# Gated delta rule: decay matrices summed in PSUM by one-hot products of split gates, beta in the exponent, one product for both decayed matrices, normalisation of two pairs at once

## The chip, the cores and the metric

The kernel runs on one core of a Trainium2 chip. The metric is the device time of one execution in microseconds (us), the median over the runs shown. A core has a matrix engine (TensorE, in the rows PE, its weight loads PEld), an elementwise engine (VectorE, DVE), an engine for functions of one operand (ScalarE, ACT), a general one (GpSimd, POOL), a queue that issues transfers (SyncE, SP) and 16 DMA engines. Operands lie in SBUF; products land in PSUM.

## The reference, cut to what matters

One layer: a bidirectional gated DeltaNet mixer, a layer norm, a mixture of experts, a second layer norm and a gate. The change lies in the mixer, 16 heads (8 pairs that share q and k), 512 tokens, forward and backward:

```python
gc = jnp.cumsum(g, axis=-1)
decay = jnp.exp(jnp.where(incl, gc[..., :, None] - gc[..., None, :], -jnp.inf))
kb = k * beta[..., None]
lhs = eye + jnp.einsum("nbhik,nbhjk->nbhij", kb, k) * decay * (1.0 - eye)
u = solve(lhs, v * beta[..., None])
w = solve(lhs, kb * jnp.exp(gc)[..., None])
attn = jnp.einsum("nbhik,nbhjk->nbhij", q, k) * decay
...
v_new = u_c - w_c @ state
o     = q_c @ state + attn_c @ v_new
state = state * gl + k_c.T @ v_new
```

After it the heads are normalised (`_rms`), multiplied by silu(z) and projected. The result is the same for both kernels.

## The kernel before

The mixer takes the first 700 us of the span, then come the first layer norm and the routing, from about 760 us the experts, whose 96 weight parts of 1 MB each stream in through a ring, and from about 1010 us the second norm and the gate. The weights of the experts can only begin to load when the mixer has given its memory back.

The mixer uses chunks of 128 tokens (4 of them). Its work goes by quarters `qt` of 2 pairs (4 heads) each:

- `projections` (`do_k`, `do_q`, `do_v`, `do_z` through `project`, L226 to L237): 24 products of 128x512 for each 128 channels, on operands that are split exactly in two fp32r parts. The split of the weights is a copy on ScalarE (L232) and a subtraction on GpSimd (L234). `conv_silu` then runs 4 taps and the silu on VectorE (L251, L255), straight out of PSUM. `do_k` also makes k k^T (L293, copied out at L295 into `kk`), `do_q` makes k q^T (L310, L313, into `kq`).
- `norms(qt)`: reciprocals and square roots per token, and `sc` = beta / |k|^2, `scd` = `sc` e^(gl - gc).
- `solve(qt)`: inverts the 32x32 blocks on the diagonal, one block a partition, by 30 steps of two VectorE operations (L389, L391); `lay(qt)` puts the result into the layouts of the products.
- `build(qt, hf)`: for 2 chunks of each direction, the decay matrices and the two decayed products E (from `kk`, for the inverse) and AT (from `kq`, for the output), then the inverse from 32 to 128 by small products. There are 8 builds. Each has 4 parts (direction, chunk) that make `dc` for 4 heads: a transfer that spreads gc over the partitions (L438), the mask added on GpSimd (L439), 4 exponentials with the bias -gc on ScalarE (L441), 2 products on GpSimd for AT (L445) and 4 on VectorE for E (L449).
- `steps(qt, hf)`: the recurrence, 8 steps for each half quarter; the product with E (L552), its two scaled copies `wd` (L558) and `w` (L562) on ScalarE, the state (L565, L569), the output (L576, L580).
- `finish(p)`: rms norm of a pair (squares L594, `rsqrt` L260 to L267, product L600), then transposes and silu(z).
- `fill`: the output projection of heads 0 to 11, through `project` too, until about 706 us; heads 12 to 15 follow chunk by chunk.

The order on each engine is made ahead of the run by a planner, which simulates the program: `weave` interleaves the parts of steps, build, finish, solve, projections and fill in the program, steps with a higher priority, and the planner takes what is ready on each engine. The engines then run in that fixed order. From the experts on the order is that of the program. The PSUM tag `pmisc` has one buffer; transposes, `kk`, `kq` and `finish` share it. All loads go through SP's one queue.

Of the kernel before, what the change touches and what calls it, by code (L numbers as in the profile page):

```python
# [16 lines left out]
P = 128  # L17
# [33 lines left out]
BKQ = 3  # L51
# [15 lines left out]
def program(ctx: ExitStack, tc: tile.TileContext, a: dict, out: bass.AP):  # L67
# [11 lines left out]
    # ---- constants  # L79
# [12 lines left out]
    # silu(y) = (1 + tanh(y / 2)) y / 2  # L92
    V.tensor_scalar(cvw, cvw, 0.5, None, op0=OP.mult)
    gdnv = c1.tile([P, 2, 32], F32, name="gdnv")
    nc.sync.dma_start(gdnv[:, 0], a["a_log"].to_broadcast([P, 32]))
    nc.sync.dma_start(gdnv[:, 1], a["dt_bias"].to_broadcast([P, 32]))
# [3 lines left out]
    negm = c1.tile([P, 2, P], F32, name="negm")  # L100
# [8 lines left out]
    hd = tr.enter_context(tc.tile_pool(name="hd", bufs=4, side="right"))  # L109
    tr2 = ExitStack()  # L110
# [28 lines left out]
    # ---- gates: g and beta, [tok, chunk, dir, head]  # L139
# [3 lines left out]
    axl = wk.tile([P, 4, NC_, 32], F32, name="th", bufs=BTH)  # L143
    ax, l1, g, gc = (axl[:, i] for i in range(4))
    V.tensor_tensor(ax, pab[:, :, 0:32], gdnv[:, 1:2, :].to_broadcast([P, NC_, 32]), op=OP.add)
# [4 lines left out]
    tmp4 = wk.tile([P, 4, NC_, 32], F32, name="zs")  # L150
    e1, u1, d1 = (tmp4[:, i] for i in range(3))
# [16 lines left out]
    V.tensor_mul(g, l1, nea.to_broadcast([P, NC_, 32]))  # L168

    # e^{gc}, e^{gl-gc}, e^{gl}  # L170
# [9 lines left out]
    ngc = sq("ngc")  # L180
    V.tensor_scalar(ngc, gc, -1.0, None, op0=OP.mult)
# [6 lines left out]
    nc.sync.dma_start(gcd, gcT)  # L188
    A.activation(egc, pg[:, 0], AF.Exp)
    A.activation(egr, pg[:, 1], AF.Exp)  # L190
    A.activation(egl, pg[:, 2], AF.Exp)
    V.tensor_scalar(negc, egc, -1.0, None, op0=OP.mult)
# [12 lines left out]
    for q in range(4):  # L205
        s = slice(32 * q, 32 * q + 32)
        V.tensor_copy(negb[s, 0], negm[s, q // 2, s])
# [5 lines left out]
    sc = sq("sc")  # L213
# [44 lines left out]
    kcm, qcm, ktm, nv, kk, kq = {}, {}, {}, {}, {}, {}  # L258

    def rsqrt(y, x, t):  # L260
        """y = 1 / sqrt(x), by Newton's steps from the exponent's half; x is lost"""
# [7 lines left out]
    def rsqrt1(y, x, t):  # L269
        """the same for one number per partition"""  # L270
# [7 lines left out]
    def do_k(p):  # L278
# [8 lines left out]
        scr = wk.tile([P, P], BF16, name="scr")  # L287
        for c in range(NC_):
            A.activation(scr, ktm[p][:, c], AF.Square, accum_out=nk2[:, c, p:p + 1])
        pk = psum.tile([P, NC_, P], F32, name="pmisc", bufs=1)  # L290
        for c in range(NC_):
            kc = kcm[p][:, c * P:(c + 1) * P]
            T.matmul(pk[:, c], kc, kc, start=(c == 0), stop=True, skip_group_check=True)  # L293
        kk[p] = hd.tile([P, NC_, P], F32, name="kk", bufs=BKK)
        A.activation(kk[p], pk, AF.Copy)  # L295

    def do_q(p):
# [6 lines left out]
        scr = wk.tile([P, P], BF16, name="scr")  # L304
# [3 lines left out]
        pk = psum.tile([P, NC_, P], F32, name="pmisc", bufs=1)  # L308
        for c in range(NC_):
# [1270 lines left out]
```

## Time and profile before

| what | us |
|---|---|
| median of 3 runs | 1121.25 |
| the 3 runs | 1120.5, 1121.25, 1128.5 |
| the profiled execution, span from its first to its last instruction | 1118.7 |
| median less that span | 2.55 |

The profile has no other time of the profiled execution than its span; what lies around it in a run is taken as the 2.55 us between that span and the median. Busy shares over the span: TensorE 90%, VectorE 75%, ScalarE 49%, GpSimd 34%. These are means over stages of different kinds, so the stages are read one by one.

### The profile page before, as it was taken

The page shows a single profiled execution, that of the slowest core. Times are in us where ns is not written, and L with a number is a line of the kernel's source. Part 1 is how long each engine was busy: PE and PEld are TensorE (multiplying, and loading weights), DVE is VectorE, ACT ScalarE, POOL GpSimd, SP SyncE. Part 2 cuts the span into 40 slices and gives each one's busy share as a digit, 9 for nine tenths or more (in the row PEclk, how much of TensorE's full clock was granted, in tenths as well). Part 3 has the DMA queues.
Part 4 walks back from the last instruction along what each step waited for, and adds up shares of the span by engine and source line. Part 5 has one row for each costly group of instructions (what it writes and reads, how often), then busy time and mean ns, then how long its engine had stood idle before and what let it go on. Part 6 is the DMA issues. An engine that isn't in the chain of part 4 may idle for free. (4 is left out here: it accounts for less than half of the span.)

```text
span 1118.7 us, 19886 instructions
## 1 busy us (share of the span) xinstructions
PE 1003.2 (90%) x6954; PEld 696.7 (62%) x6954; DVE 843.1 (75%) x1944; ACT 552.2 (49%) x1420; POOL 380.9 (34%) x337
## 2 busy tenths in 40 slices
PE   8974789887989898889998999958999999999788
PEld 7753668776767677668887887843333333333367
DVE  5899999999897879995756434597666676666794
ACT  3543467656557585735777453124543344432321
POOL 1647544336163446233541265052100000000362
PEclk8987799999899898999999999978999999999899
DMA  4423222122123212413335344868999999991411
GB/s 161 116 84 107 74 83 78 42 64 66 40 76 110 85 47 73 133 59 108 103 101 167 104 128 126 350 223 304 416 420 420 419 399 395 391 374 38 161 57 47
DMA packets 80118, 188.73 MB, mean 169 GB/s; under 512 B 15344, under 2 KB 36848, under 8 KB 67344
## 3 DMA queue, kind: packets, MB, share of 16 engines
q1 hardware_dynamic: 77712, 179.05, 44.2%
q0 software_dynamic: 2304, 8.39, 2.0%
q8 instruction: 55, 0.90, 0.3%
q14 instruction: 47, 0.39, 0.1%
HBM read 174.77 MB, written 12.65 MB: 168 GB/s over the span
## 5 line engine op out<-in xcount | busy, mean ns | idle before, releaser
L234 POOL TENSOR_TENSOR wl<-wr,wh 128x512 fp32r<-128x512 f32 x120 | 160.3, 1340 | 296.2 <-ACT wh L232 130.8
L237 PE MATMUL pin<-xh,wh 128*128 128x512 f32 x448 | 139.5, 427 | 44.7 <-DVE cv L251 28.6
L237 PE MATMUL pin<-xh,wl 128*128 128x512 f32 x448 | 132.3, 411 | 0.9 <-POOL wl L234 0.9
L237 PE MATMUL pin<-xl,wh 128*128 128x512 f32 x448 | 132.8, 414 | 0.0
L237 PEld LDWEIGHTS pin<-xh,wh 128*128 128x128 f32 x448 | 85.5, 199 | 66.2 <-issue 37.1
L232 ACT ACTIVATE wh<-wr 128x512 fp32r<-128x512 f32 x120 | 75.5, 632 | 90.8 <-PE pin L237 44.2
L1209 ACT ACTIVATE ws<-w 128x512 f32 x96 | 60.5, 630 | 112.0 <-PE ps L1214 58.7
L1207 DVE COPY ws<-w 128x512 f32 x288 | 105.6, 423 | 8.9 <-issue 3.0
L237 PEld LDWEIGHTS pin<-xl,wh 128*128 128x128 f32 x448 | 88.1, 200 | 19.0
L251 DVE SCALAR_TENSOR_TENSOR cv<-pin,cvw,cv 128x510 f32<-128x510 f32 (+1 forms) x128 | 94.6, 741 | 4.4 <-ACT cv L248 3.2
L237 PEld LDWEIGHTS pin<-xh,wl 128*128 128x128 f32 x448 | 84.5, 195 | 18.1 <-POOL wl L234 1.5
L943 POOL DMA_INDIRECT E<-x1d,gim x16 | 16.2, 1012 | 170.7 <-PE ps L1197 157.0
L449 DVE SCALAR_TENSOR_TENSOR E<-dc,sc,kk 128x128 f32<-128x128 f32 x128 | 64.9, 561 | 4.5 <-PE ps L552 2.7
L391 DVE TENSOR_TENSOR x<-x,tmp 128x30 f32<-128x30 f32 (+14 forms) x120 | 58.2, 485 | 2.1
L445 POOL TENSOR_TENSOR AT<-dc,kq 128x256 f32<-128x256 f32 x64 | 49.4, 801 | 25.9 <-PE ps L576 21.8
L389 DVE TENSOR_TENSOR tmp<-x 128x30 f32<-128x30 f32 (+14 forms) x120 | 53.8, 448 | 1.7
L1302 DVE SCALAR_TENSOR_TENSOR x<-pin,cq,x 128x512 f32<-128x512 f32 x36 | 26.9, 750 | 36.5 <-PE pin L1297 34.0
L439 POOL TENSOR_TENSOR dc<-dc,negm 128x512 f32<-128x512 f32 x32 | 44.6, 1399 | 18.3 <-DMA dc<-gcd 12.7
L576 PE MATMUL ps<-w,AT 128*128 128x128 f32 x256 | 43.2, 291 | 5.6 <-DVE oacc L580 5.6
L562 ACT ACTIVATE w<-ps,sc 128x128 f32<-128x128 f32 x128 | 40.4, 377 | 14.1 <-PE ps L552 14.0
L254 ACT ACTIVATE th<-cv 128x512 f32<-128x512 f32 x32 | 20.1, 629 | 51.9 <-DVE cv L251 32.8
L576 PEld LDWEIGHTS ps<-w,AT 128*128 128x128 f32 x256 | 39.1, 201 | 9.8 <-DVE oacc L580 6.1
(432 smaller groups left out, 2208.7 us busy)
## 6 DMA issues: line engine op xcount, KB each, us to landing
w<-in_w_gu SPq DMA_DIRECT2D x64, 1024.0 KB, 10.2
w<-in_w_dn SPq DMA_DIRECT2D x32, 1024.0 KB, 10.1
wr<-in_w_in SPq DMA_DIRECT2D x96, 256.0 KB, 2.7
dc<-gcd SPq DMA_DIRECT2D x32, 256.0 KB, 3.5
wr<-in_w_out SPq DMA_DIRECT2D x24, 256.0 KB, 2.7
zd<-th SPq DMA_DIRECT2D x16, 256.0 KB, 2.5
zs<-zd SPq DMA_DIRECT2D x16, 256.0 KB, 2.6
w<-in_pe_g SPq DMA_DIRECT2D x6, 512.0 KB, 6.9
```

The source lines that it names most:

```text
L232: A.activation(wh, wr, AF.Copy)
L234: G.tensor_tensor(wl, wr, wh.bitcast(F32), op=OP.subtract)
L237: T.matmul(ps, w[:, k], parts[k0 + k][n], start=(k0 + k + n == 0 and w is wh), stop=(k0 + k == nk_ - 1 and w is wl))
L251: V.scalar_tensor_tensor(y[:, lo:hi], ps[:, lo + j - 2:hi + j - 2], cvw[:, m, j:j + 1], y[:, lo:hi], op0=OP.mult, op1=OP.add)
L389: V.tensor_tensor(t, X[:, m + 1:, m:m + 1].to_broadcast([P, n, m]), X[:, m:m + 1, :m].to_broadcast([P, n, m]), op=OP.mult)
L391: V.tensor_tensor(X[:, m + 1:, :m], X[:, m + 1:, :m], t, op=OP.add)
L439: G.tensor_tensor(dc, dc, negm[:, d:d + 1].to_broadcast([P, 4, P]), op=OP.add)
L445: G.tensor_tensor(AT[:, k:k + 2], dc[:, 2 * pl:2 * pl + 2], kq[p][:, c:c + 1].to_broadcast([P, 2, P]), op=OP.mult)
L449: V.scalar_tensor_tensor(E[:, k + e], dc[:, 2 * pl + e], sc[:, c, hh:hh + 1], kk[p][:, c], op0=OP.mult, op1=OP.mult)
L576: T.matmul(p3[:, e], AT[:, us + e], w[:, e], start=True, stop=True, skip_group_check=True)
L1207: V.tensor_copy(ws[:, p:p + 1], src)
L1209: A.activation(ws[:, p:p + 1], src, AF.Copy)
```

## The change

The decay matrices are no longer made from transferred rows. The transposed gates are split in two fp32r parts and kept in one tile `ghl` [128, chunk, token]: partitions 0 to 31 the high part of gc, 32 to 63 its low part, 64 to 95 and 96 to 127 the two parts of log(beta), one partition for each direction and head. For each direction and pair of heads a group of 7 products adds up, in one PSUM bank `pd` [128, 2 heads, 2 chunks, 128], the mask, gc of the column token, and -gc + log(beta) of the row token; `sel` are the one-hot columns. One exponential takes all of it to SBUF, and 2 VectorE products multiply it with `kkq`, which holds kk and kq side by side, already divided by |k|^2. beta and 1/|k|^2 are then in E and AT, and `w` is a plain copy.

```diff
+    ghl = hd2.tile([P, NC_, P], F32R, name="ghl", bufs=1)
+    A.activation(ghl[0:32], gcT, AF.Copy)
+    V.tensor_tensor(ghl[32:64], gcT, ghl[0:32].bitcast(F32), op=OP.subtract)
+    ptl = psum.tile([32, NC_, P], F32, name="pmisc", bufs=1)
+    for c in range(NC_):
+        T.transpose(ptl[:, c], l1[:, c, 32:64], ident)
...
+    A.activation(lbT, ptl, AF.Copy, scale=-1.0)
+    A.activation(lbh, lbT, AF.Copy)
+    V.tensor_copy(ghl[64:96], lbh)
+    V.tensor_tensor(ghl[96:128], lbT, lbh.bitcast(F32), op=OP.subtract)
...
     def build(qt, hf, Ec, T32, T64):
-        E = ab_pool.tile([P, 16, P], F32, name="E")
-        AT = ab_pool.tile([P, 16, P], F32, name="AT")
+        EA = [ab_pool.tile([P, 8, 2, P], F32, name=n) for n in ("E", "AT")]
+        E = [t[:, :, 0] for t in EA]
...
-            for cc in range(2):
-                c = c0[d] + cc
-                dc = wk.tile([P, 4, P], F32, name="dc", bufs=3)
-                nc.sync.dma_start(dc, gcd[u0:u0 + 4, c, :][None].to_broadcast([P, 4, P]))
-                G.tensor_tensor(dc, dc, negm[:, d:d + 1].to_broadcast([P, 4, P]), op=OP.add)
-                for u in range(4):
-                    A.activation(dc[:, u], dc[:, u], AF.Exp, bias=ngc[:, c, u0 + u:u0 + u + 1])
-                for pl in range(2):
-                    G.tensor_tensor(AT[:, k:k + 2], dc[:, 2 * pl:2 * pl + 2],
-                                    kq[p][:, c:c + 1].to_broadcast([P, 2, P]), op=OP.mult)
-                    for e in range(2):
-                        V.scalar_tensor_tensor(E[:, k + e], dc[:, 2 * pl + e],
-                                               sc[:, c, hh:hh + 1], kk[p][:, c], op0=OP.mult, op1=OP.mult)
+            for pl in range(2):
+                p = 2 * qt + pl
+                u = 16 * d + 2 * p
+                pd = psum.tile([P, 2, 2, P], F32, name="pmisc", bufs=1)
+                T.matmul(pd.rearrange("p e c i -> p (e c) i"), idr, negm[:, d:d + 1].to_broadcast([P, 4, P]),
+                         start=True, stop=False, skip_group_check=True)
+                for e in range(2):
+                    T.matmul(pd[:, e], sel[:, 0, u + e:u + e + 1].to_broadcast([P, P]), ghl[:, c0[d]:c0[d] + 2],
+                             start=False, stop=False, skip_group_check=True)
+                for k in (1, 2):
+                    for cc in range(2):
+                        T.matmul(pd[:, :, cc], ghl[:, c0[d] + cc], sel[:, k, u:u + 2, None].to_broadcast([P, 2, P]),
+                                 start=False, stop=(k == 2 and cc == 1), skip_group_check=True)
+                dc = wk.tile([P, 2, 2, P], F32, name="dc")
+                A.activation(dc, pd, AF.Exp)
+                for cc in range(2):
+                    k = 4 * cc + 2 * pl
+                    V.tensor_tensor(EA[d][:, k:k + 2], dc[:, :, cc, None, :].to_broadcast([P, 2, 2, P]),
+                                    kkq[p][:, c0[d] + cc][:, None].to_broadcast([P, 2, 2, P]), op=OP.mult)
                 yield
```

Around it: log(beta) comes out of the series that makes the gates, which so runs over 64 columns a chunk instead of 32. The products for `kk` move from `do_k` into `norms`, behind the reciprocals, and both `kk` and `kq` leave PSUM by 4 scaled copies (one a chunk) instead of one:

```diff
+    def products(p, i, r):
+        pk = psum.tile([P, NC_, P], F32, name="pmisc", bufs=1)
+        for c in range(NC_):
+            cs = slice(c * P, (c + 1) * P)
+            T.matmul(pk[:, c], kcm[p][:, cs], r[p][:, cs], start=(c == 0), stop=True, skip_group_check=True)
+        for c in range(NC_):
+            A.activation(kkq[p][:, c, i], pk[:, c], AF.Copy, scale=rk2[:, c, p:p + 1])
...
     def norms(qt):
-                V.tensor_mul(sc[:, :, hs], beta[:, :, hs], rk2[:, :, ps])
-                V.tensor_mul(scd[:, :, hs], sc[:, :, hs], egr[:, :, hs])
+                V.tensor_mul(scd[:, :, hs], begr[:, :, hs], rk2[:, :, ps])
+        for p in (2 * qt, 2 * qt + 1):
+            kkq[p] = hd.tile([P, NC_, 2, P], F32, name="kkq", bufs=BKK)
+            products(p, 0, kcm)
...
     def steps(qt, hf):
-                    for e in range(2):
-                        A.activation(w[:, e], p2[:, e], AF.Copy, scale=sc[:, c, h0 + e:h0 + e + 1])
+                    A.activation(w, p2, AF.Copy)
...
-    def finish(p, sink=None):
+    def finish(qt, get):
+        ps = (2 * qt, 2 * qt + 1)
+        for p in ps:
+            for c in range(NC_):
+                for e in range(2):
+                    A.activation(scr, oacc[p][:, c, e], AF.Square, accum_out=ms[:, p % 2, c, e:e + 1])
...
+        rsqrt(f, ms, t)
+        for p in ps:
+            G.tensor_tensor(oa, oa, f[:, p % 2, :, :, None].to_broadcast([P, NC_, 2, P]), op=OP.mult)
```

`finish` so takes the squares of both pairs of a quarter and one `rsqrt` of twice the width before the first product. `T32` moves into the place of `ROW`, `dc` has 2 buffers instead of 3, `kq` and its constant `BKQ` are gone; no other constant of the planner's order is changed.

## Rows read from the trace of the kernel before

**Rows 1.** Windows of the mixer: busy us (instructions) by engine, granted clock, DMA share, GB/s.
```profile
0.00:50.00 50.00, 46.39 (x218) 37.33 (x219) 34.50 (x67) 20.52 (x43) 17.98 (x18) 0.90 0.49 149
50.00:150.00 100.00, 70.41 (x302) 55.67 (x301) 94.66 (x171) 49.90 (x139) 58.28 (x60) 0.85 0.29 87
150.00:500.00 350.00, 308.80 (x2578) 252.62 (x2577) 320.78 (x738) 218.70 (x649) 148.42 (x141) 0.94 0.23 72
500.00:700.00 200.00, 195.86 (x1395) 163.63 (x1394) 106.51 (x264) 117.80 (x338) 85.17 (x72) 0.98 0.39 120
```

**Rows 2.** Waits of TensorE (first 50 to 150 us, then 150 to 500): total, times, longest.
```profile
PE pin L237 <- DVE cv L251: 21.3, 3, 13.9
...
PE ps L565 <- ACT wd L558: 8.1, 5, 3.5
PE pin L237 <- DVE cv L251: 6.5, 4, 2.9
```

**Rows 3.** Groups by form: the build's four operations; busy, mean ns, idle before.
```profile
L449 DVE SCALAR_TENSOR_TENSOR E<-dc,sc,kk 128x128 f32<-128x128 f32 x128 | 64.9, 561 | 4.5 <-PE ps L552 2.7 <-ACT dc L441 1.7
L445 POOL TENSOR_TENSOR AT<-dc,kq 128x256 f32<-128x256 f32 x64 | 49.4, 801 | 25.9 <-PE ps L576 21.8 <-ACT kq L313 3.2 <-ACT dc L441 0.9
L439 POOL TENSOR_TENSOR dc<-dc,negm 128x512 f32<-128x512 f32 x32 | 44.6, 1399 | 18.3 <-DMA dc<-gcd 12.7 <-ACT dc L441 4.6 <-DVE tmp L389 0.9
L441 ACT ACTIVATE dc<-dc,ngc 128x128 f32<-128x128 f32 x128 | 40.8, 397 | 3.5 <-POOL dc L439 3.4
```

**Rows 4.** Five lines of VectorE: ns of one, min/median/max, first and last start.
```profile
L449 DVE SCALAR_TENSOR_TENSOR E<-dc,sc,kk x128: 332/339/2544, 66.6 to 590.9; 128x128 f32<-128x128 f32 x128
L255 DVE SCALAR_TENSOR_TENSOR cv<-th,cv x16: 676/686/1785, 69.2 to 545.5; 128x512 f32<-128x512 f32 x16
L251 DVE SCALAR_TENSOR_TENSOR cv<-pin,cvw,cv x128: 727/740/751, 28.8 to 542.7; 128x510 f32<-128x510 f32 x64, 128x511 f32<-128x511 f32 x64
L389 DVE TENSOR_TENSOR tmp<-x x120: 173/365/2075, 82.5 to 482.9; 128x30 f32<-128x30 f32 x8, 128x58 f32<-128x58 f32 x8, 128x84 f32<-128x84 f32 x8, 128x108 f32<-128x108 f32 x8
L391 DVE TENSOR_TENSOR x<-x,tmp x120: 177/368/1499, 83.3 to 484.4; 128x30 f32<-128x30 f32 x8, 128x58 f32<-128x58 f32 x8, 128x84 f32<-128x84 f32 x8, 128x108 f32<-128x108 f32 x8
```

**Rows 5.** Groups of VectorE: three of 50 to 150 us, then three of 150 to 500.
```profile
L449 DVE SCALAR_TENSOR_TENSOR E<-dc,sc,kk 128x128 f32<-128x128 f32 x32 | 18.9, 628 | 0.0
L391 DVE TENSOR_TENSOR x<-x,tmp 128x108 f32<-128x108 f32 (+14 forms) x27 | 16.2, 602 | 0.4
L389 DVE TENSOR_TENSOR tmp<-x 128x108 f32<-128x108 f32 (+14 forms) x27 | 14.8, 547 | 0.3
...
L391 DVE TENSOR_TENSOR x<-x,tmp 128x84 f32<-128x84 f32 (+14 forms) x93 | 41.9, 451 | 1.7
L389 DVE TENSOR_TENSOR tmp<-x 128x84 f32<-128x84 f32 (+14 forms) x93 | 39.0, 420 | 1.4
L449 DVE SCALAR_TENSOR_TENSOR E<-dc,sc,kk 128x128 f32<-128x128 f32 x64 | 33.4, 581 | 1.7 <-ACT dc L441 1.7
```

**Rows 6.** Groups of GpSimd from 50 to 500 us: the two that go.
```profile
L445 POOL TENSOR_TENSOR AT<-dc,kq 128x256 f32<-128x256 f32 x48 | 38.0, 820 | 17.8 <-PE ps L576 14.6 <-ACT kq L313 3.2
L439 POOL TENSOR_TENSOR dc<-dc,negm 128x512 f32<-128x512 f32 x26 | 36.2, 1398 | 18.1 <-DMA dc<-gcd 12.5 <-ACT dc L441 4.6 <-DVE tmp L389 0.9
```

**Rows 7.** TensorE, timeline: start, us, operation, count; a projection, then the gate's end.
```profile
527.80 1.07 PE L237 MATMUL pin<-xh,wl 128*128 128x512 f32 x4
528.71 1.07 PE L237 MATMUL pin<-xh,wh 128*128 128x512 f32 x4
...
1111.23 3.04 PE L1426 MATMUL pin<-w 128*128 128x256 f32 x24
```

**Rows 8.** Groups by form: scaled copies on ScalarE, and two of three in a Newton step.
```profile
L562 ACT ACTIVATE w<-ps,sc 128x128 f32<-128x128 f32 x128 | 40.4, 377 | 14.1 <-PE ps L552 14.0
L265 DVE TENSOR_TENSOR rq<-ff 128x8 f32<-128x8 f32 x24 | 9.3, 387 | 0.4
L267 DVE SCALAR_TENSOR_TENSOR ff<-rq,ff 128x8 f32<-128x8 f32 x24 | 6.0, 250 | 0.4
```

**Rows 9.** VectorE's timeline: six steps of the gates' series.
```profile
24.61 1.92 DVE L161 SCALAR_TENSOR_TENSOR th<-th,zs 128x128 f32<-128x128 f32 x6
```

More of the change, by code (lines that the diff above doesn't have):

```diff
@@ L50 @@
 BKK = 4
-BKQ = 3
 BK = 6
@@ L141, in sq @@
         return sm.tile(list(shape), F32, name=n)
-    axl = wk.tile([P, 4, NC_, 32], F32, name="th", bufs=BTH)
-    ax, l1, g, gc = (axl[:, i] for i in range(4))
-    V.tensor_tensor(ax, pab[:, :, 0:32], gdnv[:, 1:2, :].to_broadcast([P, NC_, 32]), op=OP.add)
+    axl = wk.tile([P, 2, NC_, 64], F32, name="th", bufs=BTH)
+    ax, l1 = axl[:, 0], axl[:, 1]
+    V.tensor_tensor(ax[:, :, 0:32], pab[:, :, 0:32], gdnv[:, 1:2, :].to_broadcast([P, NC_, 32]), op=OP.add)
+    V.tensor_scalar(ax[:, :, 32:64], pab[:, :, 32:64], -1.0, None, op0=OP.mult)
     beta = sq("beta")
@@ L149, in program @@
     V.reciprocal(beta, beta)
-    tmp4 = wk.tile([P, 4, NC_, 32], F32, name="zs")
-    e1, u1, d1 = (tmp4[:, i] for i in range(3))
+    eu = wk.tile([P, 2, NC_, 64], F32, name="zs")
+    e1, u1 = eu[:, 0], eu[:, 1]
+    dgt = wk.tile([P, NC_, 128], F32, name="cv")
+    d1, g, gc = dgt[:, :, 0:64], dgt[:, :, 64:96], dgt[:, :, 96:128]
     A.activation(e1, ax, AF.Abs)
@@ L192, in program @@
     V.tensor_scalar(negc, egc, -1.0, None, op0=OP.mult)
+    begr = sq("begr")
+    V.tensor_mul(begr, beta, egr)
     def diag(f):
@@ L307, in do_q @@
         V.tensor_scalar(nq2[:, :, p:p + 1], nq2[:, :, p:p + 1], EPS, EPS * P, op0=OP.add, op1=OP.mult)
-        pk = psum.tile([P, NC_, P], F32, name="pmisc", bufs=1)
-        for c in range(NC_):
-            T.matmul(pk[:, c], kcm[p][:, c * P:(c + 1) * P], qcm[p][:, c * P:(c + 1) * P],
-                     start=(c == 0), stop=True, skip_group_check=True)
-        kq[p] = hd2.tile([P, NC_, P], F32, name="kq", bufs=BKQ)
-        A.activation(kq[p], pk, AF.Copy)
+        products(p, 1, qcm)
     def do_v(h):
@@ L502, in build @@
             for u in range(8):
-                T.matmul(pq[s, u], E[f, 8 * d + u, s], T64[f, c0[d] + u // 4, u % 4], start=True, stop=True,
+                T.matmul(pq[s, u], E[d][f, u, s], T64[f, c0[d] + u // 4, u % 4], start=True, stop=True,
                          skip_group_check=True)
@@ L575, in steps @@
                     for e in range(2):
[L576 removed]
+                        T.matmul(p3[:, e], EA[d][:, us + e, 1], w[:, e], start=True, stop=True, skip_group_check=True)
                     if n == 0:
@@ new lines, in finish @@
+    def finish(qt, get):
+        ps = (2 * qt, 2 * qt + 1)
+        ms = wk.tile([P, 2, NC_, 2], F32, name="ms")
+        scr = wk.tile([P, P], BF16, name="scr", bufs=1)
+        for p in ps:
[3 more added lines that the diff above has]
+        for p in ps:
+            V.scalar_tensor_tensor(ms[:, p % 2], ms[:, p % 2], 1.0 / P, nq2[:, :, p:p + 1].to_broadcast([P, NC_, 2]),
+                                   op0=OP.mult, op1=OP.add)
+        f = wk.tile([P, 2, NC_, 2], F32, name="ff")
+        t = wk.tile([P, 2, NC_, 2], F32, name="rq2")
+        rsqrt(f, ms, t)
+        for p in ps:
+            oa = oacc[p]
+            G.tensor_tensor(oa, oa, f[:, p % 2, :, :, None].to_broadcast([P, NC_, 2, P]), op=OP.mult)
+        for p in ps:
+            oa = oacc[p]
+            for e in range(2):
+                h = 2 * p + e
+                pt = psum.tile([P, NC_, P], F32, name="pmisc", bufs=1)
+                for c in range(NC_):
+                    T.transpose(pt[:, c], oa[:, c, e], ident)
+                zs = wk.tile([P, S], F32, name="zs")
+                nc.sync.dma_start(zs, z_dram[h])
+                V.scalar_tensor_tensor(zs, pt.rearrange("p c t -> p (c t)"), nw, zs, op0=OP.mult, op1=OP.mult)
+                if p not in get():
+                    nc.sync.dma_start(oz_dram[h], zs)
+                else:
+                    oh, ol = get()[p][e]
+                    A.activation(oh, zs, AF.Copy)
+                    V.tensor_tensor(ol, zs, oh.bitcast(F32), op=OP.subtract)
+            yield
@@ L694, in program @@
         if hf == 0 and qt:
-            ws.append((2, parts(lambda p: finish(p, sink.get(p)), (2 * qt - 2, 2 * qt - 1)), 0, 0, 0.5))
+            ws.append((2, finish(qt - 1, lambda: sink), 0, 0, 0.5))
         if k == 6:
@@ L760, in program @@
         early_p.append(((lambda w, p: w, 1), 256 * n, 256, pt_))
-    lng = [hd.tile([P, S], F32, name="kk", bufs=BKK) for _ in range(4)]
+    lng = [hd.tile([P, S], F32, name="kkq", bufs=BKK) for _ in range(4)]
     for i in range(4):
         nc.sync.dma_start(lng[i], a["ln"][:, i // 2, 512 * (i % 2):512 * (i % 2) + 512].to_broadcast([P, 512]))
-    weave((2, parts(lambda p: finish(p, o4[2 * p - 12:2 * p - 10]), (6, 7)), 0, 0, 0.2), (4, split_w2(), 0, 0, 0.5),
+    weave((2, finish(3, lambda: {6: o4[0:2], 7: o4[2:4]}), 0, 0, 0.2), (4, split_w2(), 0, 0, 0.5),
           (8 - F7, fl, 0, 0, 1))
```

96 lines of the change are left out of this document (35 added, 61 removed).

## The prediction

> **What bounds the kernel now.** I cut the mixer into stretches first, because the busy shares of the page are means over stages with different limits [rows 1]. Up to 50 us it loads. From 50 to 150 us VectorE is busy for 94.7 of 100 us and TensorE for 70.4. From 150 to 500 us VectorE has 320.8 of 350 us (92%) and TensorE 308.8 (88%). From 500 to 700 us TensorE has 195.9 of 200 (98%) and VectorE 106.5. So VectorE ends last in the first stretch, both engines share the second, and TensorE ends last in the third. The change touches no stage behind the mixer, and the output projection (TensorE) ends the mixer: what it gains or loses up to 700 us moves the rest of the span by as much.
>
> The waits say the same. From 50 to 150 us TensorE waits 21.3 us for the convolution's taps on VectorE to free its PSUM buffers; from 150 to 500 us its idle time, 350 - 308.8 = 41.2 us, is in small pieces, the longest sums behind `wd` on ScalarE and again behind the taps [rows 2]. Most of those pieces end with VectorE, which is nearly full.
>
> Last I looked at what makes VectorE slow. The E product on 128x128 (L449) takes 339 ns in the median but 561 in the mean, up to 2544; the taps, which read PSUM, stay between 727 and 751 [rows 4]. So operations on two SBUF operands are stretched and the others are not. The stretching goes with GpSimd: the solve's two lines take 602 and 547 ns while GpSimd is busy 58% of the time, 451 and 420 at 42% [rows 1, 5]. GpSimd's L439 and L445 are 74.2 of its 206.7 us between 50 and 500 us, 36% [rows 1, 6].
>
> **The change part by part.** There are 8 builds; by the counts of L449, 32 and 64 of 128, 2 lie in 50 to 150 us, 4 in 150 to 500 and 2 after it [rows 5]. A build now has 4 groups, so 8, 16 and 8 groups.
>
> *GpSimd, ScalarE and SP.* 94 us of GpSimd go [rows 3]. On ScalarE 128 exponentials of 397 ns go, 32 wide ones come; the 64 copies of `w` of 128x256 cost at most the two of 377 ns that they replace; `kk` and `kq` cost 64 copies of about 377 ns instead of 16 wider ones [rows 3, 8]. ScalarE ends with less work, and it has 131 us spare in 150 to 500 us [rows 1]; I price it at 0 by itself. The 32 transfers of `dc` and their places in SP's queue go too; TensorE's listed waits name no transfer, so this is 0 as well.
>
> *TensorE.* A group is one product of 512 columns and 6 of 256, in fp32r. A 512 one starts every (528.71 - 527.80)/4 = 0.23 us; 256 ones with a new weight each take 3.04/24 = 0.127 with the last one's drain, and half a 512 one is 0.115; I take 0.12 [rows 7]. So a group is 0.23 + 6 x 0.12 = 0.95 us, 32 are 30.4: 7.6, 15.2 and 7.6 us by stretch. No row shows these one-hot products; by the nearest, 4 x 0.23 = 0.92 us (its 2048 columns as four of 512) and 0.23 + 6 x 0.127 = 0.99 us bound a group.
>
> *VectorE.* 128 E products become 64 of 128x512 with two SBUF operands. Without disturbance such a one takes 686 ns (L255); stretched as L449 is, 561/339, it would take 1.13 us [rows 3, 4]. With about a third less of GpSimd beside it I take 0.87, near the lower end: 64 x 0.87 = 56 against 64.9. For 50 to 150 us that is 16 x 0.87 = 14 against 18.9 (-5, between -8 and -1), for 150 to 500 us 32 x 0.87 = 28 against 33.4 (-6, between -11 and +3). The other operations are stretched less. For the solve's lines the excess over the medians 365 and 368 is, by stretch, 27 x (0.18 + 0.23) = 11 us and 93 x (0.055 + 0.083) = 13 us [rows 4, 5]; 36% of it is 4 and 5 us. By the slope between the stretches (127 and 151 ns for 16 points of GpSimd's share) a loss of 26 points in the first, with both lines' full stretching gone, would give 12. I take -10 and -8, which counts the transposes, copies and the silu, too. `finish` halves its Newton steps, of 4 x 9 operations of 0.25 to 0.39 us (-11 us, 6 of them before 500 us) [rows 8], and `norms` loses 16 small ones (-1 and -2). So VectorE: -16 and -22 us.
>
> *The gates' start.* Some 14 operations of a dependent chain get twice the columns, at 0.32 us each now [rows 9]: 0 to 4.5 us later, I take +3. The work for log(beta) and `ghl` isn't needed by `solve(0)`. That the products for `kk` now wait for `norms(0)` I price at 0, since VectorE has other work all that time [rows 1]; the 8 copies of 0.377 us would be 3 us if it had none [rows 8].
>
> *50 to 150 us.* VectorE ends last here, and the solve is a chain on it: -16, bounds -24 and -4. TensorE's 70.4 + 7.6 = 78 us fit in 84, the more as its granted clock is 0.85 in this stretch and 0.98 where it is kept busy [rows 1].
>
> *150 to 500 us.* VectorE falls to 299 us, TensorE rises to 324. TensorE would so be first, and what counts is its idle time of 41.2 us. If none of it goes the stretch takes 324 + 41 = 365 (+15). If it goes down to the 2% of the last stretch, 331 (-19). Two things end it, VectorE's and ScalarE's queues, and both get shorter: VectorE's spare share rises from 8% to 13%. I take the idle time as halved: 324 + 20 = 344, -6.
>
> *TensorE's headroom.* By the rows on matmuls TensorE is at 88% there, by its weight loads at 252.6 of 350 us, 72% [rows 1]. The Trainium skill, Perfetto Trace Analysis, section Identifying the Most-Contended Engine, says that matmul occupancy is a poor measure of how near the engine is to its limit, and that weight loads' busy share is a better one. By that rule VectorE stays first and this stretch would give its -22 us instead of my -6; what speaks against it is that matmuls alone fill 98% from 500 us on, with nothing between them.
>
> *After 500 us.* TensorE is full: 8 groups are +7.6, less what falls into its 4 us of idle time: +6, bounds 0 and +8. The second `rsqrt` that `finish` saves and the squares that it now takes first change places beside projections that keep TensorE full to the end; that is 0. Without that cover the eight squares of the second pair would come ahead of the first pair's product, at about 0.4 us each (the nearest copy is 0.377 [rows 8]) some 3 us.
>
> Sum: +3 - 16 - 6 + 6 = -13. Against the profiled execution 1118.7 - 13 = 1105.7; with the 2.55 us between it and the median, 1108.
>
> **The rivals.**
>
> *TensorE gives the gain back.* The idle time between 150 and 500 us isn't VectorE's making but that of the recurrence's chain (product, copy on ScalarE, product, state on VectorE), as the wait behind `wd` suggests. Then that stretch is +9 to +15 and the sum +3 - 16 + 10 + 6 = +3: 1124, no change. The same comes if the new products are stretched as L449 was. For it: VectorE's spare time is small and yet TensorE idles. Against: the waits named for VectorE are the more numerous.
>
> *TensorE pays in full (slower).* The groups sit in `pmisc`, a single buffer that the transposes, `kk`, `kq` and `finish` use too. In the planner's fixed order a group whose exponential is late holds all of TensorE's queue behind it: the steps' products and with them VectorE. Then the idle time between 50 and 500 us, 29.6 + 41.2 = 70.8 us, stays as it is, and all 30.4 us and the 3 of the start are added: 1155. It decides as soon as less than 22 us of the 70.8 go (33.4 - 22 = 11 us, 1%). Against: `pmisc` is behind none of the larger waits now [rows 2].
>
> *VectorE was all of it.* TensorE's matmuls are pipelined and its busy time holds gaps that the groups fill, so that VectorE alone sets the stretch up to 500 us and the groups after it cost nothing: +3 - 16 - 22 + 0 = -35, 1086. For it: its weight loads fill only 72% [rows 1]. Against: the full last stretch. The page named above would have it so.
>
> **How the numbers follow.** A measurement of this kernel can tell about 1% (11 us) from no change. My forecast has 0.35, around 1108 with 1095 to 1115 of its own; the gain given back 0.31; paid in full 0.22; VectorE all of it 0.12. Faster by over 1% is the first and the last, 0.47; within 1% 0.31; slower 0.22. The range leaves out about a tenth at each end: 1084 to 1134. With all terms at their lower bounds (0, -24, -19, 0) the median would be 1078, at their upper ones (4.5, -4, +15, +8) 1145.
>
> **What would show it.** Right: L449's successor near 0.87 us with a maximum well above its median; the solve's lines under 0.5 us in the first stretch; the first steps some 13 us earlier; TensorE at 94% between the first solve and the full stretch; the granted clock above 0.85 in the first. Wrong: waits of TensorE that name `pmisc` or the exponential of `dc`, groups of over 1.1 us, or an idle time before 500 us that stays near 70 us. Then the added products have become the bound, and the forecast fails at the halved idle time.

## The result, and the profile after

The changed kernel takes 1185.6 us (median, 1185.2 to 1185.9) where the kernel before took 1124.6: a ratio of 1.054 (95% interval 1.049 to 1.058), 61 us slower. The forecast was 1108, its range 1084 to 1134. The nearest case on record was "TensorE pays in full", 1155, and the time lies above that too.

The profiled execution has a span of 1183.4 us, against 1118.7 before. The page's first part, busy time by engine, of after:

```profile
PE 1063.7 (90%) x7182; PEld 750.1 (63%) x7182; DVE 795.8 (67%) x1831; ACT 534.8 (45%) x1311; POOL 289.5 (24%) x242
```

VectorE lost 47 us and GpSimd 91, as the change intends. TensorE has 60 us more, which is twice the 30 us that the groups were reckoned at. The windows of the same stretches as [rows 1], with one more, since the mixer now ends later:

```profile
0.00:50.00 50.00, 40.05 (x172) 32.18 (x173) 30.09 (x73) 17.22 (x31) 12.04 (x15) 0.82 0.34 115
50.00:150.00 100.00, 79.19 (x472) 63.35 (x471) 86.42 (x163) 47.34 (x124) 34.33 (x30) 0.82 0.22 65
150.00:500.00 350.00, 319.35 (x2368) 265.72 (x2367) 275.31 (x614) 196.10 (x556) 105.28 (x96) 0.93 0.18 58
500.00:700.00 200.00, 181.97 (x1420) 148.50 (x1418) 97.35 (x227) 104.10 (x285) 37.48 (x30) 0.90 0.28 86
700.00:770.00 70.00, 69.37 (x352) 57.85 (x350) 23.75 (x54) 25.17 (x68) 31.51 (x24) 0.98 0.39 117
```

From 150 to 500 us VectorE is down from 320.8 to 275.3 us, and yet fewer matmuls were done than before (2368 against 2578, groups included). From 500 to 700 us TensorE is no longer full: 182.0 of 200 us, at a granted clock of 0.90 where it was 0.98. The projections that were done at 705.6 us before now end at 760.7; 55 of the 65 us between the spans lie in the mixer, and the first steps even start earlier. These rows (shortest, median and longest ns; first and last start) answer to [rows 4] and [rows 8]: the decayed products, the first transposes behind a solve, and the steps' copies of `w`.

```profile
L476 DVE TENSOR_TENSOR E<-dc,kkq x32: 676/685/1781, 108.9 to 630.5; 128x512 f32<-128x512 f32 x32
L476 DVE TENSOR_TENSOR AT<-dc,kkq x32: 678/684/1756, 116.3 to 651.4; 128x512 f32<-128x512 f32 x32
...
L428 DVE STREAM_TRANSPOSE x<-x x4: 1961/2045/2167, 127.2 to 515.1; 128x1024 f32<-128x1024 f32 x4
...
L588 ACT ACTIVATE w<-ps x64: 362/384/423, 165.6 to 721.5; 128x256 f32<-128x256 f32 x64
```

The same two lines in the kernel before:

```profile
L404 DVE STREAM_TRANSPOSE x<-x x4: 2153/2213/2304, 155.6 to 484.6; 128x1024 f32<-128x1024 f32 x4
...
L562 ACT ACTIVATE w<-ps,sc x128: 346/370/464, 194.6 to 654.1; 128x128 f32<-128x128 f32 x128
```

The first `w` is copied at 165.6 us, where it was 194.6. The last one is copied at 721.5, where it was 654.1. So the steps take 556 us instead of 460. The loss in the mixer is neither in the gates nor in the first solve; it is the pace of everything behind them. The other 10 us between the spans lie behind the last projection, which leaves 422.7 us where it left 413.1; no run takes those apart.

One row shows what TensorE did from 50 us to the last projection. First the kernel before, then after:

```profile
50.00:705.60 655.60, 580.66 (x4298) 476.46 (x4297) 522.48 (x1172) 386.54 (x1125) 293.04 (x271) 0.94 0.29 89
```

```profile
50.00:760.70 710.70, 640.58 (x4557) 527.71 (x4556) 478.00 (x1049) 370.88 (x1026) 208.60 (x178) 0.91 0.23 71
```

Busy 580.7 became 640.6 (+59.9) and idle time 74.9 became 70.1 (-4.8). The groups bring some 30 us of products at the full clock. Some 6 us are work that stood in the first 50 us before (46.4 us busy there, 40.1 now). The rest, about 24 us, is the clock: a mean of 0.91 over 710.7 us is (1 - 0.91) x 2 x 710.7 = 128 us at the half level, against 79 us before; a group takes 1.0 us at the full and 1.9 us at the half level (the two timelines further below), so about half of these 49 us, 24, is time that the clock added.

### The profile page after: what moved, and what is told of

Same layout as the page of the kernel before. It is cut to its first block, busy times and chain, and to the rows that moved or that the text cites. A ratio compares the mean times of both kernels' runs of the same rounds, so it can differ in the third digit from the quotient of the medians.

```text
span 1183.4 us, 19925 instructions
## 1 busy us (share of the span) xinstructions
PE 1063.7 (90%) x7182; PEld 750.1 (63%) x7182; DVE 795.8 (67%) x1831; ACT 534.8 (45%) x1311; POOL 289.5 (24%) x242
## 5 line engine op out<-in xcount | busy, mean ns | idle before, releaser
L261 PE MATMUL pin<-xl,wh 128*128 128x512 f32 x448 | 136.3, 421 | 0.0
L261 PEld LDWEIGHTS pin<-xh,wh 128*128 128x128 f32 x448 | 88.5, 205 | 46.6 <-issue 13.1
L261 PEld LDWEIGHTS pin<-xh,wl 128*128 128x128 f32 x448 | 87.9, 200 | 18.0
L567 DVE SCALAR_TENSOR_TENSOR r<-ps,negc,nv 128x128 f32<-128x128 f32 x96 | 29.1, 344 | 41.2 <-PE ps L564 31.0
L1460 PE MATMUL ps<-w 128*128 128x512 f32 (+1 forms) x192 | 44.2, 391 | 0.0
L1248 PE MATMUL pin<-ws,AT 128*32 128x512 f32 x256 | 39.1, 593 | 3.1 <-DVE ws L1241 3.1
L585 ACT ACTIVATE wd<-ps,scd 128x128 f32<-128x128 f32 x96 | 29.9, 365 | 24.8 <-PE ps L579 23.8
L1460 PEld LDWEIGHTS ps<-w 128*128 128x128 f32 x192 | 35.9, 198 | 6.9
L1248 PE MATMUL pin<-w,AT 128*32 128x512 f32 x256 | 38.8, 602 | 0.0
## 6 DMA issues: line engine op xcount, KB each, us to landing
w<-in_w_gu SPq DMA_DIRECT2D x64, 1024.0 KB, 11.6
w<-in_w_dn SPq DMA_DIRECT2D x32, 1024.0 KB, 11.6
```

Source lines behind the costliest of these rows:

```text
L261: T.matmul(ps, w[:, k], parts[k0 + k][n], start=(k0 + k + n == 0 and w is wh), stop=(k0 + k == nk_ - 1 and w is wl))
L567: V.scalar_tensor_tensor(r[:, e], p1[:, 0, e], negc[:, c, h0 + e:h0 + e + 1], nv[p][:, c, e], op0=OP.mult, op1=OP.add)
L585: A.activation(wd[:, e], p2[:, e], AF.Copy, scale=scd[:, c, h0 + e:h0 + e + 1])
L1248: T.matmul(ps[32 * j:32 * j + 32], l[:, 32 * j:32 * j + 32], w[:, j], start=first, stop=last, skip_group_check=True)
L1460: T.matmul(pg[n][:, 0:w], x_[:, kt], w_[kt][:, 512 * n + o:512 * n + o + w], start=(kt == 0 and m == 0), stop=(kt == KT - 1 and m == 2))
```

## The experiments

Three theories stood at the start. A: the groups' time on TensorE is paid in full. B: the single buffer `pmisc` is what costs. C: another edit costs (normalisation, gates, copies). Every ratio is to the kernel before in the same session, whose median lies between 1123.2 and 1127.9 us in them; the idle times and clocks of both kernels and of eleven runs are in a table at the end of this section.

**e1, the groups made twice.** In the kernel after, the seven products of a group are issued two times into the same buffer.

```diff
+for _ in range(2):
     T.matmul(pd..., idr, negm[:, d:d + 1]...)      # and the six others
```

> The changed kernel with the 7 products of each of the 32 groups made twice (the second pass overwrites the first), nothing else. Theory A, the groups' time on TensorE is paid in full: a second pass adds what a first one costs, 0.95 us at the full granted clock to 1.9 at the half one, 30 to 60 us over 32 groups, so 1215 to 1245 us. Theory B, the single pmisc buffer and the exponential behind it are the cost, not the products: pmisc is held about 1 us longer of some 3 us, a third of the 61 us lost, so about 1205. Theory C, the cost lies in the other edits (kk behind the norms, wider gates, both pairs in finish) and the products run in idle time: within 1% of 1186.

1213.3 us, ratio 1.083 (1.075 to 1.091): 28 us over after, 0.87 us for each of 32 additional groups (33 us by the ratios). So in the changed kernel a group more is a group paid. But this tells only the marginal price, and a second pass holds the buffer longer as well, so it doesn't separate A from B; it explains about 28 to 33 of the 61 us.

**e2, unread groups in the kernel before.** Its decay rows, decayed products and normalisation stay as they were; 32 groups that nobody reads go into `pmisc` (and `T32` lies in the place of `ROW`, as in after).

```diff
+pd = psum.tile([P, 2, 2, P], F32, name="pmisc", bufs=1)
+T.matmul(pd..., idr, ...)                          # seven products, not read
 dc = wk.tile([P, 4, P], F32, name="dc", bufs=3)
```

> The kernel before with the 32 groups of 7 products added to pmisc in the places where the builds make dc, on copies of the identity; nothing reads them, dc is made from rows as before. Theory A: 30 to 55 us more than before, 1152 to 1180. Theory B: no exponential holds the buffer, so the groups only take gaps, 0 to 15 us more. Theory C: within 1% of before.

1163.3 us, ratio 1.038 (1.030 to 1.045), 40 us. That is what A expects, and more than the 30 us of products; B's 0 to 15 fails for groups that hold the buffer only while they are written.

**e3, the groups in two buffers.** One line of the changed kernel: the groups go to `ps1`, a tag of two buffers that the products of the builds and steps use too.

```diff
-pd = psum.tile([P, 2, 2, P], F32, name="pmisc", bufs=1)
+pd = psum.tile([P, 2, 2, P], F32, name="ps1")
```

> The changed kernel with pd in the tag ps1 (two buffers, shared with the builds' and steps' products) instead of pmisc (one buffer). Theory A: the same products, 1175 to 1195. Theory B: most of the loss goes, 1125 to 1155. Theory C: 1186 within 1%.

1130.7 us, ratio 1.006 (1.002 to 1.010): 55 of the 61 us are gone, as B has it. The same row of TensorE as above:

```profile
50.00:701.90 651.90, 602.60 (x4556) 504.88 (x4556) 476.17 (x1047) 364.56 (x1017) 207.33 (x178) 0.96 0.25 78
```

The profiled execution took 1123.1 us, 7.6 less than the median of e3's ten runs, so its row shows e3 at its best. The matmuls are the same (4556 against 4557), and they take 38.0 us less busy time. The half level takes (1 - 0.96) x 2 x 651.9 = 52 us instead of 128, and half of these 76 us is 38. That fits better than it can be read: a hundredth of the clock is 13 to 14 us of half level, and some of the half level is idle time. Idle time falls from 70.1 to 49.3 us, another 20.8. Together that is the difference of 58.8 us between the two stretches. Where the groups stand shows what the buffer does to the order. TensorE's timeline, the four first products of one build, in after and then in e3:

```profile
153.62 0.50 PE L463 MATMUL pmisc<-negm,idr 128*128 128x512 f32 x1
...
165.00 0.40 PE L463 MATMUL pmisc<-negm,idr 128*128 128x512 f32 x1
...
176.47 0.48 PE L463 MATMUL pmisc<-negm,idr 128*128 128x512 f32 x1
...
196.09 0.47 PE L463 MATMUL pmisc<-negm,idr 128*128 128x512 f32 x1
```

```profile
159.37 0.50 PE L463 MATMUL ps<-negm,idr 128*128 128x512 f32 x1
...
165.27 0.50 PE L463 MATMUL ps<-negm,idr 128*128 128x512 f32 x1
...
166.28 0.40 PE L463 MATMUL ps<-negm,idr 128*128 128x512 f32 x1
...
169.91 0.40 PE L463 MATMUL ps<-negm,idr 128*128 128x512 f32 x1
```

The four groups span 42.5 us with one buffer and 10.5 with two. The other builds agree: over the second to the eighth, first and last group lie 46 us apart on average in after and 16 in e3. Half of a build's first small products (L497), those of one direction, can run before the last group, and in this build of after some do, at 174.81 us; the other direction's can't, and the steps of its half need the whole build.

**e7, e2's unread groups in two buffers.** The same one line, in e2.

> The kernel before with 32 unread groups of seven products, now in the tag of two buffers (in the single buffer they made it 1163). If the cost there was the buffer: 1123 to 1138, a few us for what of the 32 us of products finds no idle TensorE. If TensorE's time itself is paid: 1150 to 1163.

1135.3 us, ratio 1.006 (1.003 to 1.009), 7 us where e2 had 40. So e2's 40 us weren't A after all: TensorE's time for 32 groups costs some 7 us in the kernel before (3 to 10 by the interval), and the buffer costs 33 us even where nobody reads the groups.

**e4, VectorE's relief without the groups.** The changed kernel with its decay rows brought by transfers and masked on GpSimd as before; the exponentials take -gc + log(beta) as their bias, and one product makes `E` and `AT`.

```diff
-T.matmul(pd..., idr, ...)                          # seven products
-A.activation(dc, pd, AF.Exp)
+nc.sync.dma_start(dc, gcd[u0:u0 + 4, c, :]...)
+G.tensor_tensor(dc, dc, negm[:, d:d + 1]..., op=OP.add)
+A.activation(dc[:, u], dc[:, u], AF.Exp, bias=ngb[:, c, u0 + u:u0 + u + 1])
```

> The changed kernel with dc made as before (rows by transfer, mask on GpSimd, 4 exponentials whose bias now holds -gc + log beta); everything else of the change stays: kkq with one VectorE product for both decayed matrices, plain copy of w, kk behind the norms, wider gates, finish by two pairs. Theories A and B: the 32 groups are gone from TensorE and pmisc, the relief of VectorE stays, 1095 to 1125. Theory C: still above 1165.

1130.7 us, ratio 1.007 (1.004 to 1.011). No theory had this. VectorE is relieved by half of what after has (500.0 us in the stretch of the table below, 522.5 before, 478.0 in after), and TensorE's idle time stays at 74.1 us:

```profile
50.00:713.60 663.60, 589.55 (x4346) 484.87 (x4345) 500.00 (x1045) 383.69 (x1113) 252.99 (x210) 0.94 0.30 90
```

ScalarE's waits and then GpSimd's, from 50 to 700 us (total, times, longest), say where the relief may end:

```profile
ACT dc L446 <- POOL dc L444: 20.8, 12, 4.9
```

```profile
POOL dc L444 <- DMA dc<-gcd: 23.7, 10, 5.3
```

The exponentials wait 20.8 us for the mask, which waits 23.7 us for the transfer; before, these were 3.4 and 12.7 [rows 3]. So this much relief of VectorE shows no gain as long as the rows come by transfer. That it is worth nothing by itself isn't shown: e4 keeps the later gates (the row of `gcd` is sent at 44.3 us, before at 39.0) and the batched normalisation.

**e12, the rows by products alone.** The kernel before, with the mask and four one-hot products into two buffers of PSUM in place of transfer and mask; `E` and `AT` as before, `dc` in two buffers instead of three.

```diff
-nc.sync.dma_start(dc, gcd[u0:u0 + 4, c, :]...)
-G.tensor_tensor(dc, dc, negm[:, d:d + 1]..., op=OP.add)
+pd = psum.tile([P, 4, P], F32, name="ps1")
+T.matmul(pd, idr, negm[:, d:d + 1]...)
+T.matmul(pd[:, u], sel[:, u0 + u:u0 + u + 1]..., ghl[:, c]...)      # u = 0 to 3
```

> The kernel before, its decay rows made in two buffers of PSUM by five products a chunk of a direction (the mask and four one-hot products; as many columns as the three-product groups) in place of the transfer and GpSimd's mask; the two decayed products, beta and the normalisation as before, the exponentials read PSUM, two buffers of decay rows in place of three. If the transfer and the mask on GpSimd's queue are what held the kernel before: 1102 to 1115. If VectorE's products must go too for the gain: 1122 to 1138.

1117.3 us, ratio 0.992 (0.989 to 0.994). Between the two expectations. TensorE's busy time rises by 17.5 us and its idle time falls by 18.7, to 56.2:

```profile
50.00:704.40 654.40, 598.20 (x4436) 495.21 (x4436) 504.38 (x1169) 377.67 (x1113) 248.25 (x236) 0.94 0.26 78
```

VectorE's products stayed, but its busy time didn't: 504.4 us, 18 less than before and near e4's 500.0, beside a GpSimd that has lost its mask. So e12 isn't free of relief; what it has and e4 hasn't is rows without transfer and mask. The first copies of `w` say the same, in e4 and in e12:

```profile
L561 ACT ACTIVATE w<-ps x64: 361/383/519, 193.4 to 654.0; 128x256 f32<-128x256 f32 x64
```

```profile
L576 ACT ACTIVATE w<-ps,sc x128: 350/370/513, 170.7 to 647.8; 128x128 f32<-128x128 f32 x128
```

With rows by products the steps begin 24 us earlier than before (194.6), with rows by transfer 1 us. In e2, by transfer too, they begin 13 us earlier, at 181.6, so the order alone moves them as well.

**e8, three products in a group.** e3, with the part that varies down the partitions as the bias of four exponentials. The four products for it go, and with them the rows of log(beta) and their selectors.

```diff
-for k in (1, 2):
-    for cc in range(2):
-        T.matmul(pd[:, :, cc], ghl[:, c0[d] + cc], sel[:, k, u:u + 2, None]...)
-A.activation(dc, pd, AF.Exp)
+for e in range(2):
+    for cc in range(2):
+        A.activation(dc[:, e, cc], pd[:, e, cc], AF.Exp, bias=ngb[:, c0[d] + cc, u + e:u + e + 1])
```

> The changed kernel with the groups in the tag of two buffers and three products in a group in place of seven: the part that varies down the partitions comes as the bias of four exponentials of 128x128 instead. TensorE loses half of the groups' columns, about 16 us of 32 at full clock. If the two-buffer version is set by TensorE's time: 1114 to 1123. If the groups' products there lie in idle time of TensorE, or ScalarE's longer exponentials take its place: 1128 to 1138.

1105.0 us, ratio 0.978 (0.973 to 0.983), faster than either kernel, and more than TensorE's 16 us.

```profile
50.00:682.20 632.20, 594.47 (x4432) 493.83 (x4433) 474.21 (x1047) 381.09 (x1111) 207.21 (x178) 0.95 0.26 81
```

TensorE is busy 94% of this stretch and idle for 37.7 us, half of before.

**e11, e8 with the four products put back.** Their selectors are zero, so they add nothing and take the same columns.

> The three-product groups in two buffers, with the four products put back in each as products whose selectors are zero there; the bias stays with the exponentials, and the log-beta rows stay out. If TensorE's time is what the four products cost: 1121 to 1132. If their absence was worth nothing and the shorter chain of the gates or the order made the gain: 1103 to 1110.

1118.8 us, ratio 0.993 (0.991 to 0.996). Against e8's 0.978 the four products cost 1.5%, 17 us (11 to 23 by the two intervals), near the 16 us of their columns at the full clock. So with two buffers more time on TensorE is paid. That its columns alone are the price isn't shown: in the table the stretch is 23 us longer, 12.7 of them busy and 10.6 idle, and behind the last projection e11 is 6 us shorter than e8. Between e11 and e3 lie another 1.3%, with the same columns: the log(beta) rows with their flips and copies, or the order of the one wide exponential. These two I didn't tell apart.

**e10, e8's groups back in the single buffer.** The word of e3, reversed.

> The three-product groups, put back in the single buffer. If the single buffer is what costs, whatever the products in a group: 1135 to 1165. If the buffer's cost comes from the length of the seven products that hold it: 1110 to 1130.

1195.5 us, ratio 1.061 (1.057 to 1.065): 90 us for the buffer. With half of the products, and a longer hold by ScalarE (four exponentials of 375 ns in place of one of 597), it is worse than after. The length of the products isn't what makes the buffer dear; the hold as a whole grew with the exponentials. Between the traces of e10 and e8 lie 92 us, 72 of them up to the last projection and 20 behind it.

**e13, e8's groups in the other single buffer.** `ps3`, which in the mixer only the steps' last products use.

> The three-product groups in the other single buffer of PSUM, ps3, whose only other tenants in the mixer are the last products of the steps. If one buffer is too few for the groups, whoever shares it: 1160 to 1200, as in pmisc (1195.5). If what costs in pmisc is the line of tenants there (the projections' flips and products of keys, queries and values, the normalisation's flips), which take the buffer in the order of the program text: 1100 to 1125.

**e14, e10 with the neighbours moved.** The four tenants of `pmisc` that belong to the projections go to `ps1`, the groups stay.

> The three-product groups in the single buffer pmisc, and its four tenants of the projections (flips of keys, queries and values, products of keys and queries) moved to the tag of two buffers. If one buffer is too few for the groups: 1160 to 1200. If the line of tenants costs: 1100 to 1130, unless the tenants bring the line with them to the buffers of the steps, which would show as the same long mixer with the steps waiting for their first product.

1169.9 us, ratio 1.041 (1.035 to 1.047), and 1170.2 us, ratio 1.041 (1.035 to 1.046). Both are slower than before. Of the 90 us about 65 stay in another single buffer as well as in `pmisc` without the projections, so they go with one buffer for groups that must be written, read by ScalarE and released one after the other; the 25 that e10 has more go with sharing `pmisc`'s line with the projections. The expectation of e14 left open that the moved tenants would bring the line to the steps; as a wait that doesn't show, since the steps' first products (L554) wait for 2.7 us in all. The distance between a build's groups marks the single buffer without measuring its price: over the same builds it is 16 us in e8, 50 in e10 and 71 in e14, and e14 is the faster of the last two.

**e5, e6, e9, the normalisation.** e5 is the kernel before with the batched normalisation alone; e6 is e3 and e9 is e8 with the normalisation pair by pair, as before.

```diff
-ws.append((2, finish(qt - 1, lambda: sink), 0, 0, 0.5))
+ws.append((2, parts(lambda p: finish(p, sink.get(p)), (2 * qt - 2, 2 * qt - 1)), 0, 0, 0.5))
```

> The kernel before with the batched normalisation alone (both pairs of a quarter squared, normalised and flipped together). If the batching is off the path, as the theories of the groups' time and of the single buffer have it: 1118 to 1128 us, as before. If the batching is what eats the relief of VectorE (it holds the pair's sums until both are ready): 1130 to 1140.

> The changed kernel with the groups in the tag of two buffers and the normalisation pair by pair, as before. If the batching costs nothing: 1128 to 1134, as the two-buffer version measured (1130.7). If the batching eats the relief: 1112 to 1122.

> The three-product groups in two buffers (1105.0 us, ratio 0.978 to before) and the normalisation pair by pair. If pair by pair is worth what the seven-product versions showed, 1.4% between them: 1087 to 1096, a ratio of 0.963 to 0.970. If that 1.4% was the order that the planner happened to write: 1098 to 1112.

e5 1121.2 us, ratio 0.993 (0.990 to 0.996); e6 1120.1 us, 0.992 (0.990 to 0.995); e9 1097.7 us, 0.975 (0.972 to 0.979). Batching makes the kernel before 0.7% faster, while taking it out makes e3 1.4% faster and e8 0.3%, which lies within the two intervals. So the edit has no price that can be added up; that it shifts the planner's order, by about a per cent in either direction, is my guess. Theory C is not what made the change slow. e9 is the fastest version that ran.

TensorE from 50 us to the last projection, each line from one row like those above:

| kernel | ratio | stretch, us | busy | idle | clock |
|---|---|---|---|---|---|
| before | 1 | 655.6 | 580.7 | 74.9 | 0.94 |
| after | 1.054 | 710.7 | 640.6 | 70.1 | 0.91 |
| e2, unread groups, one buffer | 1.038 | 687.5 | 616.6 | 70.9 | 0.94 |
| e7, unread groups, two buffers | 1.006 | 669.8 | 599.7 | 70.1 | 0.95 |
| e4, relief, no groups | 1.007 | 663.6 | 589.6 | 74.1 | 0.94 |
| e12, rows by products alone | 0.992 | 654.4 | 598.2 | 56.2 | 0.94 |
| e3, seven products, two buffers | 1.006 | 651.9 | 602.6 | 49.3 | 0.96 |
| e11, three and four of zeros | 0.993 | 655.5 | 607.2 | 48.3 | 0.95 |
| e8, three products, two buffers | 0.978 | 632.2 | 594.5 | 37.7 | 0.95 |
| e9, e8 by pairs | 0.975 | 631.6 | 590.1 | 41.5 | 0.97 |
| e10, three, in `pmisc` | 1.061 | 704.0 | 626.5 | 77.5 | 0.90 |
| e13, three, in `ps3` | 1.041 | 680.3 | 617.0 | 63.3 | 0.92 |
| e14, three, neighbours moved | 1.041 | 693.7 | 619.9 | 73.8 | 0.91 |

## Why the prediction was wrong

**VectorE's part was right in size.** The decayed product has a median of 685 ns and a mean of 754 and 784 ns, where 0.87 us was taken and 0.69 to 1.13 allowed. The solve's lines, which were to come under 0.5 us in the first stretch, take 458 and 387 ns in these groups of VectorE from 50 to 150 us:

```profile
L415 DVE TENSOR_TENSOR x<-x,tmp 128x30 f32<-128x30 f32 (+14 forms) x30 | 13.7, 458 | 0.9
L413 DVE TENSOR_TENSOR tmp<-x 128x30 f32<-128x30 f32 (+14 forms) x30 | 11.6, 387 | 0.8
L476 DVE TENSOR_TENSOR AT<-dc,kkq 128x512 f32<-128x512 f32 x4 | 2.6, 685 | 0.0
L476 DVE TENSOR_TENSOR E<-dc,kkq 128x512 f32<-128x512 f32 x4 | 2.6, 684 | 0.0
```

The first steps came 29 us earlier, for the 13 of the forecast. I had 16 wide products in that stretch; there are 8, because the groups come late: 5.2 us in place of the 18.9 of [rows 5], and the other 8, some 5 us, were only moved. That the earlier steps are VectorE's doing, as the forecast had it, isn't shown: e4 has VectorE busy for 87.0 us of the first stretch and no earlier steps, e12 for 95.8 and steps 24 us earlier. And the excess over the medians 365 and 368 was not all stretching, since these lines run over widths from 30 to 240.

**The gates' start** came 7.7 us later for the 3 taken (the row of `gcd` is sent at 46.7 us, before at 39.0). 43.3 in e3, which has the same gates, shows that some 3 of it differ with the order or the execution.

**A group's own time was right at the full clock only.** The timeline of TensorE has one from 309.89 to the projection behind it at 310.90, 1.01 us for the 0.95 reckoned:

```profile
309.89 0.50 PE L463 MATMUL pmisc<-negm,idr 128*128 128x512 f32 x1
310.23 0.40 PE L466 MATMUL pmisc<-ghl,sel 128*128 128x256 f32 x2
310.46 0.61 PE L470 MATMUL pmisc<-sel,ghl 128*128 128x256 f32 x4
310.90 0.63 PE L261 MATMUL pin<-xh,wh 128*128 128x512 f32 x2
```

The first build, at 105 us, shows the other case, with what each group waited for in brackets:

```profile
108.70 0.50 PE L463 MATMUL pmisc<-negm,idr 128*128 128x512 f32 x1 [1.23 <-ACT nv L347]
...
110.56 0.60 PE L463 MATMUL pmisc<-negm,idr 128*128 128x512 f32 x1 [0.69 <-ACT dc L473]
110.95 0.63 PE L466 MATMUL pmisc<-ghl,sel 128*128 128x256 f32 x2
111.38 1.06 PE L470 MATMUL pmisc<-sel,ghl 128*128 128x256 f32 x4
113.17 0.80 PE L463 MATMUL pmisc<-negm,idr 128*128 128x512 f32 x1 [0.73 <-ACT dc L473]
```

Each of these groups waits for ScalarE to release the one buffer, and the one at 110.56 takes 1.9 us, at the half level. I had said the granted clock would rise above 0.85 in this stretch; it is 0.82.

**The step that failed is the idle time "taken as halved".** It stayed: 70.1 us for 74.9. The forecast's terms make a stretch of 655.6 - 13 = 642.6 us up to the last projection, 580.7 + 30.4 = 611.1 busy and 31.5 idle. The measured one is 68 us longer: 38.6 of them are idle time that didn't go, and 29.5 are busy time that the forecast put at nothing, some 24 of it the clock of all products and some 6 the work moved out of the first 50 us. The 9.6 us more behind the last projection it put at nothing too. By the windows the idle time before 500 us did fall, to 20.8 + 30.7 = 51.5 us from 70.8, so that sign didn't come as worded; the work had slipped behind the mark, and from 500 to 700 us there are 18.0 us where 4.1 were. The reason given for the halving, that VectorE's and ScalarE's queues end the idle time and that both get shorter, is wrong in two ways. With rows by transfer VectorE's relief doesn't shorten it (e4, with half of that relief: 74.1). Taking the rows off the transfer and GpSimd's mask does (e12: 56.2), and both together halve it (e8: 37.7), but only with two buffers (e10: 77.5). In e3, the change as it is with two buffers, it is 49.3, a third less.

**The rival that came nearest was priced too low and argued against for the wrong reason.** "TensorE pays in full" named the single buffer `pmisc`, a group whose exponential is late, and an idle time that stays. Its price was the groups' products at the full clock. What it lacked is the clock: the same matmuls are 38 us longer in after than in e3, about half of the difference in half-level time between them. The reason against it, that `pmisc` is behind none of the larger waits [rows 2], was no evidence: the kernel before has no tenant there that ScalarE must read before TensorE may go on within one build. Even in after, TensorE's waits that name `pmisc` come to 11.6 us; these are the largest three:

```profile
PE pmisc L320 <- ACT scr L333: 2.3, 1, 2.3
PE pmisc L638 <- DVE zs L641: 2.2, 3, 1.0
PE pmisc L463 <- ACT kkq L322: 1.5, 2, 1.2
```

Most of the cost isn't a wait at the buffer; what the traces show changed is the order around it, 42.5 us between a build's first and last group. That this order is the planner's answer to the single buffer, and that it makes the cost, is my reading of e3, e13 and e14, not shown: the planner's list itself wasn't changed with the buffer held fixed.

The Trainium skill has the rule that I passed over: Perfetto Trace Analysis, section Optimizing Tensor Performance, says that independent matmul groups should rotate through different PSUM banks, so that one's evacuation overlaps the next group's matmuls. The runs agree that two buffers pay, with 55 us in the pair of after and e3 and 90 us in that of e10 and e8; that the gain is the overlap the rule names they don't show.

**"TensorE gives the gain back" fails in its number**, 1124, and the idle time that it gives to the recurrence's chain falls with two buffers (e3). But its first half, that the idle time isn't VectorE's making, is what e4 shows, and it is near e3's result, 1130.7, where the groups' products eat what the idle time gives back.

**"VectorE was all of it" fails.** Where only four products of zeros are added, from e8 to e11, the kernel takes 17 us more, for 16 us of columns. The rule of the Trainium skill, Perfetto Trace Analysis, section Identifying the Most-Contended Engine, that weight loads' share shows TensorE's headroom better than matmuls', would have left room there: 493.8 of 632.2 us in e8, 78%. As far as this one pair tells, the matmuls' 94% was the truer measure.

**The normalisation**, priced at -11 us of VectorE, is not visible as such: -0.7% alone and the other sign in e3.

## What to carry to other kernels

Before a product is moved into PSUM, count the buffers of its tag and who must read one before the next can be written: here 32 groups of 1 us in a buffer that ScalarE has to release cost 55 to 90 us more than in two buffers, and no larger wait in the trace of the kernel before points at it. When an engine is relieved, follow the chain to the next late thing (here the rows' transfer and mask) and ask whether that goes too; here the relief without it lost 0.7% (e4), the rows by products without the rest of the change gained 0.8% (e12), and the two together gained 2.2% (e8). And when TensorE loses its density, price the clock for all of its products, not for the new ones alone.

## What the hardware showed

By the records TensorE can be busy all the time and stay at the half level. Two windows of after, with its busy time first and the granted clock third from the end:

```profile
438.00:448.00 10.00, 10.00 (x54) 7.74 (x53) 4.15 (x13) 5.59 (x19) 1.20 (x4) 0.52 0.08 28
540.00:561.00 21.00, 21.00 (x174) 16.88 (x173) 11.27 (x26) 10.96 (x30) 1.03 (x2) 0.52 0.01 2
```

The second begins behind a wait of 2.28 us for ScalarE:

```profile
539.53 1.16 PE L320 MATMUL pmisc<-qcm,kcm 128*128 128x128 f32 x8 [2.28 <-ACT scr L333]
```

It then holds small products of 32x32 and 64x64, steps' products and one group, without a gap in the records, at 0.52 for 21 us. The records' ends of matmuls are modelled, so that idle moments inside a product wouldn't show. I had not expected a clock that low at a full busy share. What kept it down the rows don't show, and no run here was made for it.
